# A strip of the last store in three transfers, three quarters of it on eight engines

## Chip, core and metric

One NeuronCore of a Trainium2 chip (trn2). The metric is the device time of one execution in microseconds (us). The profile's span is some 1.8 us shorter than that time. All executions compared below are fast ones, at a granted clock of 1.0; the one exception is named where it comes.

## The reference

```python
x = np.random.randn(32, 3, 256, 256).astype(np.float32)
np.rot90(x, k=2, axes=(-2, -1))       # every 256 x 256 image turned by 180 degrees
```

Turning an image by 180 degrees is the same as reversing its 65,536 values. Input and output have 25.17 MB each. There is no arithmetic: the kernel moves bytes and reverses them.

## The kernel before

The 96 images are cut into three tiles A, Bt and Ct of 32 images (8 MB). An image lies on four partitions, a quarter (E = 16,384 values, 64 KB) on each. The copies reverse every row inside its partition. The store writes the four quarters of an image in turned order. All transfers are issued by SyncE.

```python
    G = 32                      # images in a tile
    E = L // 4                  # 16384 values, 64 KB: one row of a partition
    J = E // 8                  # 2048, columns of one copy
    N = E // 32
    # x4: g (n s) e  (128 rows of 64 KB);   o4: g n s e  (32 images, 4 quarters)

    def load(t, g, lo=0, hi=E):
        nc.sync.dma_start(out=t[:, lo:hi], in_=x4[g][:, lo:hi])

    def store(t, g):
        nc.sync.dma_start(out=o4[g][:, ::-1, :], in_=t[:, :])

    def inside(t):              # 12 copies on VectorE: reverse each row in place
        ...

    load(A, 0, 0, N)            # 2 KB of each row first
    load(A, 0, N, E)
    load(Bt, 1)
    load(Ct, 2)
    for g, t in enumerate((A, Bt, Ct)):
        inside(t)
        store(t, g)
```

## Time and profile before

| | kernel before |
|---|---|
| time | 122.92 us, median of 3 runs (122.79 to 123.21) |
| span of the profile | 121.1 us |
| DMA engines busy | 97.4% of 16 engines' span |
| VectorE busy | 36% |
| last store: issued, landed | 77.6 us, 120.3 us |

The lines themselves are in the prediction below. The trace keeps a record of every packet (start, duration, bytes), and each transfer ends on each of its engines with a packet of 4 bytes (9 ns), and a count of the transfer's semaphore follows it; I call that packet the *closing*. The kernel before has 112 of them for its seven transfers, 16 each, and 16 counts on the semaphore of its last store. A packet starts 3 to 4 ns before the one ahead of it on the same engine ends, and so an engine's packets can be strung together, although a record does not name its engine. Where two engines coincide to a few ns, they can be mistaken for each other.

### The profile page before, as it was taken

The numbers are of one execution on the slowest core, as the hardware profiler recorded it, in microseconds if no ns is written. First come the engines' busy times: TensorE is split into PE (matmuls) and PEld (weight loads), VectorE is DVE, ScalarE is ACT, GpSimd is POOL, SyncE is SP. The second block draws the span as 40 slices with busy tenths as digits, with TensorE's granted clock in tenths as the row PEclk, the third lists the DMA queues.
The fourth block names the chain that finished last, engine by engine and source line by source line (L and its number), as shares of the span: only waits on it lengthen the run. The fifth ranks groups of instructions, "written<-read, shape, count | busy, mean of one in ns | idle before, by whom it ended". The sixth has DMA issues, their size and how long they took to land.

```text
span 121.1 us, 94 instructions
## 1 busy us (share of the span) xinstructions
DVE 44.2 (36%) x36; POOL 0.2 (0%) x4
## 2 busy tenths in 40 slices
DVE  0000000599994199998039999600000000000000
POOL 0000000000000000000000000000000000000000
DMA  9977987897799879978989977997799779977980
GB/s 359 399 336 336 650 356 336 346 693 346 346 411 628 346 346 476 563 346 346 346 346 476 563 346 346 563 476 346 346 584 455 346 346 606 433 346 346 671 368 0
DMA packets 1008, 50.33 MB, mean 416 GB/s; under 512 B 112, under 2 KB 112, under 8 KB 240
## 3 DMA queue, kind: packets, MB, share of 16 engines
q1 hardware_dynamic: 1008, 50.33, 97.4%
HBM read 25.17 MB, written 25.17 MB: 416 GB/s over the span
## 4 chain that ended last, share of the span: by engine, by line
DMA 33%; DVE 25%; another core or an unknown queue 4%; issue 1%; SPq 1%; DVEq 0%
DMA Bt<-in_x_dram 33%; DVE T L53 8%; DVE Ct L53 8%; DVE Bt L53 8%; SPq L56 1%; DVEq L53 0%
## 5 line engine op out<-in xcount | busy, mean ns | idle before, releaser
L53 DVE COPY T<-A 128x2048 f32<-128x2048 f32 x4 | 4.9, 1227 | 22.7 <-DMA A<-in_x_dram 22.6
L53 DVE COPY T<-Ct 128x2048 f32<-128x2048 f32 x4 | 4.9, 1227 | 5.4 <-DMA Ct<-in_x_dram 5.3
L53 DVE COPY T<-Bt 128x2048 f32<-128x2048 f32 x4 | 4.9, 1227 | 4.4 <-DMA Bt<-in_x_dram 4.3
L53 DVE COPY Bt<-T 128x2048 f32<-128x2048 f32 x4 | 4.9, 1227 | 0.1
L53 DVE COPY A<-T 128x2048 f32<-128x2048 f32 x4 | 4.9, 1227 | 0.1
L53 DVE COPY Ct<-Ct 128x2048 f32<-128x2048 f32 x4 | 4.9, 1227 | 0.1
L53 DVE COPY Bt<-Bt 128x2048 f32<-128x2048 f32 x4 | 4.9, 1227 | 0.1
L53 DVE COPY A<-A 128x2048 f32<-128x2048 f32 x4 | 4.9, 1227 | 0.1
L53 DVE COPY Ct<-T 128x2048 f32<-128x2048 f32 x4 | 4.9, 1227 | 0.1
L89 POOL MEMSET const-bfloat16-1.0<- 128x1 bf16 x1 | 0.1, 101 | 0.0
L89 POOL MEMSET const-uint8-127<- 128x1 uint8 x1 | 0.1, 101 | 0.0
L89 POOL MEMSET const-float32-0.0<- 128x1 f32 x1 | 0.1, 98 | 0.2 <-issue 0.2
L89 POOL MEMSET const-float32-1.0<- 128x1 f32 x1 | 0.1, 98 | 0.0
## 6 DMA issues: line engine op xcount, KB each, us to landing
A<-in_x_dram SPq DMA_DIRECT2D x1, 7936.0 KB, 21.4
A<-in_x_dram SPq DMA_DIRECT2D x1, 256.0 KB, 2.8
Bt<-in_x_dram SPq DMA_DIRECT2D x1, 40.3
Ct<-in_x_dram SPq DMA_DIRECT2D x1, 60.3
out_dram<-A SPq DMA_DIRECT2D x1, 43.9
out_dram<-Bt SPq DMA_DIRECT2D x1, 43.8
out_dram<-Ct SPq DMA_DIRECT2D x1, 42.7
```

The source lines that it names most:

```text
L53: tc.keep_in_program_order(nc.vector.tensor_copy(out=dst, in_=src))
L56: nc.sync.dma_start(out=t[:, lo:hi], in_=x4[g][:, lo:hi])
L89: nc = _bacc.Bacc("TRN2", target_bir_lowering=False, num_devices=1)
```

## The change

The intent, as the diff shows it: take 1 KB off the end of each of the 128 rows of the last store, and send these pieces in three transfers that don't use the engines evenly. 64 rows go in 16 groups, twice 32 rows in 8 groups. Eight engines carry 4 + 4 + 4 of the 1 KB pieces and the other eight carry 4. If the first eight end the last store early, this levels them.

```diff
+    M = E // 64                     # 256 values, 1 KB
...
-    def store(t, g):
-        nc.sync.dma_start(out=o4[g][:, ::-1, :], in_=t[:, :])
+    def store(t, g, lo=0, hi=E, i=0, j=G):
+        nc.sync.dma_start(out=o4[g][i:j, ::-1, lo:hi], in_=t[4 * i:4 * j, lo:hi])
...
-    for g, t in enumerate((A, Bt, Ct)):
-        inside(t)
-        store(t, g)
+    inside(A)
+    store(A, 0)
+    inside(Bt)
+    store(Bt, 1)
+    inside(Ct)
+    store(Ct, 2, 0, E - M)
+    store(Ct, 2, E - M, E, 0, 16)
+    store(Ct, 2, E - M, E, 16, 24)
+    store(Ct, 2, E - M, E, 24, 32)
```

## The prediction

> **What bounds the kernel now.** I read four views, in this order: the page's busy shares with its DMA part, the DMA issues, the waits of SyncE's queue, and the stretches of time at the very end.
>
> ```profile
> DVE 44.2 (36%) x36; POOL 0.2 (0%) x4
> ...
> DMA packets 1008, 50.33 MB, mean 416 GB/s; under 512 B 112, under 2 KB 112, under 8 KB 240
> ...
> q1 hardware_dynamic: 1008, 50.33, 97.4%
> ```
>
> VectorE works a third of the span. The 16 DMA engines work 97.4% of it, all from one queue. Every byte has to go in once and out once (25.17 MB each way), so this is a copy at the pace of the DMA engines, and the chain of waits on the page (which names the load of Bt and the copies) is only one of several paths beside it.
>
> ```profile
> out_dram<-A SPq DMA_DIRECT2D x1, 43.9
> out_dram<-Bt SPq DMA_DIRECT2D x1, 43.8
> out_dram<-Ct SPq DMA_DIRECT2D x1, 42.7
> ```
>
> ```profile
> 77.59 0.54 SPq L59 DMA_DIRECT2D out_dram<-Ct  x1
> ```
>
> The last store is issued at 77.59 us (timeline) and lands 42.7 us later, at 120.3, although its own 8 MB take only 19.3 us: it stands behind the stores of A and Bt in the queue. So whatever SyncE issues shortly after 77.6 is issued some 20 us before an engine could start on it.
>
> ```profile
> SPq L100 <- DMA out_dram<-Bt: 19.3, 1, 19.3
> SPq L100 <- DMA out_dram<-Ct: 19.3, 1, 19.3
> SPq L100 <- DMA out_dram<-A: 3.5, 1, 3.5
> ```
>
> At the end SyncE only waits: 19.3 us for the store of Bt, 19.3 us more for that of Ct. The engines run from one 8 MB transfer into the next without a gap, and the end is set by the slowest of 16 engines.
>
> ```profile
> 119.20:119.40 0.20, 0.00 (x0) 0.00 (x0) 1.00 0.00 0
> 119.40:119.50 0.10, 0.00 (x0) 0.00 (x0) 1.00 0.01 0
> 119.50:119.60 0.10, 0.00 (x0) 0.00 (x0) 1.00 0.02 0
> 119.60:119.70 0.10, 0.00 (x0) 0.00 (x0) 1.00 0.01 0
> 119.70:119.80 0.10, 0.00 (x0) 0.00 (x0) 1.00 0.03 0
> 119.80:119.90 0.10, 0.00 (x0) 0.00 (x0) 1.00 0.02 0
> 119.90:120.00 0.10, 0.00 (x0) 0.00 (x0) 1.00 0.01 0
> 120.00:121.10 1.10, 0.00 (x0) 0.00 (x0) 1.00 0.00 0
> ```
>
> This is the part that the change aims at. The last but one column is the DMA share; this view books a packet at one moment, so what is seen here are only the 4-byte packets with which each engine closes the transfer (9 ns each). They are spread over 119.4 to 120.0. In the packet records of the trace the 16 closings end at 119.44, .51, .55, .61, .62, .66, .75, .75, .75, .76, .78, .83, .85, .86, .88 and 119.98; their mean is 119.73. The semaphore counts the last of them 0.34 us after it (120.32), and the barriers that follow end the span 0.8 us after that. If all 16 ended together the span could shrink by 119.98 - 119.73 = 0.25 us, 0.2% of the time. That is the ceiling of any balancing of this store. The records do not say which engine a packet ran on, so which engines are the late ones can't be read.
>
> [...] a 64 KB packet takes 2418 ns, 27.1 GB/s, 434 for 16. [...] Here it is 1.0 us from the first issue (0.73) to the first packet (1.75), and 0.34 us from the last packet to the semaphore; between queued transfers neither is seen. [...]
>
> **The change part by part.** *Duration of a packet.* The trace has three sizes in steady flow: 2 KB 84 ns, 62 KB 2342, 64 KB 2418. (2418 - 84) / 62 = 37.65 ns per KB, and 84 - 2 x 37.65 = 8.7 ns fixed; 62 KB gives 2343, as measured. A packet starts some 3 ns before the one ahead of it ends. So I estimate 1 KB at 46 ns, a pitch of 43, and 63 KB at 2380. A closing packet adds some 6 ns.
>
> *Removed.* 1 KB from each of 128 rows, 8 rows per engine: 8 x 37.65 = 0.30 us less on every engine.
>
> *Added.* The strips of 64, 32 and 32 rows: 4 rows on every engine from the first, 4 + 4 more on engines 0 to 7. Engines 0 to 7: 12 x 43 ns + 3 x 6 ns = 0.53 us. Engines 8 to 15: 4 x 43 + 6 = 0.18 us. Net: engines 0 to 7 end 0.23 us later, engines 8 to 15 end 0.12 us earlier; the mean moves by +0.06 us, which is what the cutting costs.
>
> *Moved.* Nothing in the copies or loads. SyncE issues three more transfers, each some 0.4 to 0.54 us (the seven issues now take 0.39 to 0.63), until about 79.4 us: hidden, as shown above. At the end it has three more semaphores to pass; a wait that is already satisfied costs some 0.05 us (from the last landing to the next instruction it is 0.07 now), perhaps one of them after the last landing.
>
> *What lies on the path.* Only the last closing counts, and it depends on where engines 0 to 7 stand in the list above. (a) They are the 8 early ones: their last goes from 119.75 to 119.98, the others' last from 119.98 to 119.86; the change is 0.0. (b) They are mixed: drawing 8 of the 16 at random, the last closing moves by 0.17 us on average. (c) They are the late ones: +0.23. SyncE's issue of a transfer takes 0.39 us and the first packets of the 16 engines start over 0.36 us[...]. But the first reads took from 81 to 620 ns, which shuffles the order. I take (a) 45%, (b) 45%, (c) 10%: 0.45 x 0 + 0.45 x 0.17 + 0.1 x 0.23 = 0.10 us. [...] The end's waits: 0.03. Sum +0.18 us on 122.92: 123.1.
>
> **Rivals.** *The balance works.* Best case: engines 0 to 7 are the early ones by just the right amount, and the last closing falls by perhaps 0.1 us: 122.8. For it: the spread of 0.54 us is there. Against it: half of the 0.35 us shifted between the halves falls on engines that differ among themselves as much as the halves can; in the list the 8 early ones themselves span 0.31 us, so two groups can't level it.
>
> *A new wait.* The strips write between the rows' ends of the range of the main store. If the program takes the two for overlapping, SyncE waits until the main store has landed (120.3) before it issues the strips: 3 issues of 0.45, 1.0 us to the first packet, 0.2 us of data, 0.34 to land: +2.5 to 3 us, 125.7. Against it: the two pieces of A's load, which also interleave column-wise, are issued at 0.73 and 1.18 with no wait between; but there it is the SBUF side that they share, and the DRAM side only as a read. I give it 3%.
>
> *Small writes to HBM are slow.* 1 KB packets may not keep a pitch of 43 ns: the first 2 KB reads took up to 620 ns. Once running, they took 84. If a 1 KB write cost 100 ns, engines 0 to 7 would end 12 x 57 = 0.7 us later still: 123.8.
>
> *The strips go first.* The columns of the strip are final after the second copy on Ct (65 us), so the order on SyncE's queue could be turned round. Each engine would then carry the same packets in another order: no change of the time.
>
> **Range and chances.** Three runs of the kernel before lie within 0.42 us, more than the effect. Below: the good rival and that scatter, 122.6. Above: slow small packets or the wrong half, 123.6. Also, at 58 us all 16 engines once took 3.2 to 3.8 us for a 64 KB packet, 1.1 us lost; the three runs agree so well that I take it to be in all of them. Faster by over 2% means below 120.5: impossible with an unchanged byte count and 0.25 us to win, 0.01. Slower by over 2% is above 125.4: only the new wait does it, 0.03.
>
> **What would show it.** Packets 1008 + 128 + 32 = 1168, 144 of them under 512 B and 272 under 2 KB. Three issues more, done by about 79.5 us. 1 KB packets of about 46 ns. Of the 144, 16 + 8 + 8 close the strips; it would be 160 if all three used 16 engines. The last closing within -0.1 to +0.4 us of 119.98. I am wrong if SyncE issues a strip after 120 us, if 1 KB packets take 100 ns or more, if the strips of 32 rows use other than 8 engines, or if a gap opens between transfers.

Where a recorded text said of the hardware what no trace or run shows, the passage is cut and the cut marked. One cut took a term out of the sum: +0.18 us was 0.10 for the engines, 0.05 for a longer first strip (cut) and 0.03 for the end's waits. Without the cut term it would be +0.13 us, 123.05.

That a strip of 8 groups goes to eight engines was assumed: the trace before has only transfers with 16 closings. The changed kernel's trace shows 8 for each such strip. Which of the 16 engines these are stands in no record: "engines 0 to 7" in the recorded texts is a name for them and not a measured number. Below they are *the eight*, and the rest *the other eight*.

## The result

| | before | after |
|---|---|---|
| median of 4 runs | 122.94 us (122.79 to 123.21) | 122.99 us (122.96 to 123.14) |
| span of the profile | 121.1 us | 121.2 us |
| last closing (packet records) | 119.98 us | 119.99 us |
| last closing counted by its semaphore | 120.31 us | 120.33 us |

The ratio is 1.0004 with a 95% interval of 0.9985 to 1.0023: no difference that could be told. A ratio here and below is the mean time of one kernel's fast runs over that of the other's fast runs of the same rounds, so it isn't quite the ratio of the medians quoted.

The page of the changed kernel, with the packets and the queue:

```profile
DVE 44.2 (36%) x36; POOL 0.2 (0%) x4
...
DMA packets 1169, 50.33 MB, mean 415 GB/s; under 512 B 145, under 2 KB 273, under 8 KB 401
...
q1 hardware_dynamic: 1168, 50.33, 97.4%
q14 instruction: 1, 0.00, 0.0%
```

The kernel's queue has the 1168 packets that were worked out in advance; the 1169th (24 bytes) is in the queue that the page calls "instruction", and it is also the one too many in each of the three counts of small packets. Of the 145, then, 144 are closings: 112 of seven transfers on 16 engines, 16 for the strip of 64 rows and 8 for each strip of 32. The engines' share is what it was.

Its DMA issues (name, issuing queue, count, KB of each, us to landing):

```profile
out_dram<-Ct SPq DMA_DIRECT2D x1, 8064.0 KB, 42.4
...
out_dram<-Ct SPq DMA_DIRECT2D x1, 64.0 KB, 42.0
out_dram<-Ct SPq DMA_DIRECT2D x2, 32.0 KB
```

Its timeline on SyncE (start, duration):

```profile
77.66 2.93 SPq L62 DMA_DIRECT2D out_dram<-Ct  x4
```

All four pieces are issued between 77.66 and 80.59 us, 40 us before they land. In the instruction records the strips take 0.74, 0.79 and 0.71 us to issue against 0.54 us for the main part: longer than I had assumed, and quite hidden.

The waits of SyncE's queue (line, releaser, us in total, times, longest):

```profile
SPq L109 <- DMA out_dram<-Bt: 19.3, 1, 19.3
SPq L109 <- DMA out_dram<-Ct: 19.2, 1, 19.2
...
SPq L109 <- DMA out_dram<-A: 1.2, 1, 1.2
```

Nothing new waits: still 19.3 us and then 19.2 us for transfers that run back to back. The wait for A's store is shorter by 2.3 us (1.2 against 3.5) only because SyncE comes to it later, having issued more.

The end, in stretches of 0.1 us (the last columns are the DMA share and GB/s; a packet is booked whole where it starts):

```profile
119.20:119.30 0.10, 0.00 (x0) 0.00 (x0) 1.00 0.51 164
119.30:119.40 0.10, 0.00 (x0) 0.00 (x0) 1.00 0.61 205
119.40:119.50 0.10, 0.00 (x0) 0.00 (x0) 1.00 0.82 277
119.50:119.60 0.10, 0.00 (x0) 0.00 (x0) 1.00 0.69 226
119.60:119.70 0.10, 0.00 (x0) 0.00 (x0) 1.00 0.31 103
119.70:119.80 0.10, 0.00 (x0) 0.00 (x0) 1.00 0.22 72
119.80:119.90 0.10, 0.00 (x0) 0.00 (x0) 1.00 0.18 62
119.90:120.00 0.10, 0.00 (x0) 0.00 (x0) 1.00 0.04 10
120.00:121.20 1.20, 0.00 (x0) 0.00 (x0) 1.00 0.00 0
```

Where the kernel before showed only its closings, the small packets are now visible. The engines still stop one after another: a staircase that falls from 0.8 at 119.45 to nothing at 120.0, at the same moment as before. The spread has stayed (the last closings of the 16 engines lie within 0.59 us, against 0.54 before), and so has the end.

Who stopped when? Only eight engines have three strips, so a chain of packets with three tells them from the others. In this execution the eight closed the main part at 119.04, .06, .06, .06, .12, .25, .34 and .47 (mean 119.17), the other eight at 119.23, .29, .39, .39, .41, .49, .54 and .74 (mean 119.44). So the eight really were early, by 0.26 us in the mean. But the last of them trailed its own half by 0.3 us. After the strips the last of the eight ends at 119.99, the last of the other eight at 119.92. Without the cut, the latter would have closed at about 119.74 + 0.30 = 120.04 (an estimate from 8 KB at 37.65 ns each). The levelling thus gained about 0.05 us in this execution. Behind it stands an instruction that was not there before: SyncE's wait for the last strip ends with the count at 120.33 (0.34 us after the closing; 0.32 to 0.40 in the ten traces), and it passes one more, satisfied, wait before it goes on to the end of the program: in the instruction records it gets there 0.13 us after the last count, where it took 0.08 before. That is 0.04 us more. None of these small steps is larger than the scatter from one execution to another: the four profiled kernels in which no store is cut (the one before, and `e5_no_copies_b`, `e6_two_turns` and `e8_swap` below) have their last closing at 119.98, 120.05, 119.89 and 120.09 us.

### The profile page after: what moved, and what is told of

Read it like the earlier page. It is cut to its first block, busy times and chain, and to the rows that moved or that the text cites. A ratio compares the mean times of both kernels' runs of the same rounds, so it can differ in the third digit from the quotient of the medians.

```text
span 121.2 us, 97 instructions
## 1 busy us (share of the span) xinstructions
DVE 44.2 (36%) x36; POOL 0.2 (0%) x4
## 3 DMA queue, kind: packets, MB, share of 16 engines
q1 hardware_dynamic: 1168, 50.33, 97.4%
## 4 chain that ended last, share of the span: by engine, by line
DMA 33%; DVE 24%; another core or an unknown queue 4%; issue 1%; SPq 1%; DVEq 0%
DMA Bt<-in_x_dram 33%; DVE T L56 8%; DVE Bt L56 8%; DVE Ct L56 8%; SPq L59 1%; DVEq L56 0%
```

## The experiments

The theory: 16 engines, none of which pauses between two transfers (99.0% busy from 3 to 119 us in the kernel before), each with a list of packets; the end comes when the slowest list is done. The change shifts 0.35 us from one half to the other, while each half is itself spread by some tenths of a us. The rivals are in the expectations. "Before" in the first four had a median of 122.89 us (122.78 to 123.86, 11 runs in those rounds).

### Cutting without shifting

```diff
     store(Ct, 2, 0, E - M)
-    store(Ct, 2, E - M, E, 0, 16)
-    store(Ct, 2, E - M, E, 16, 24)
-    store(Ct, 2, E - M, E, 24, 32)
+    store(Ct, 2, E - M, E)
```

> The strip as one transfer of 128 rows on all 16 engines: the cutting without the shift. Theory (the slowest engine's packets set the end): each engine gains 8 x (43 - 37.65) + 6 = 0.05 us of packet work, and SyncE perhaps one more wait of 0.06 us at the end: 122.94 + 0.05 to 0.11 = 123.0 to 123.05 us; 8 packets of 1 KB of 46 ns on every engine; the spread of the 16 closings stays some 0.5 to 0.7 us, as without a cut. Rival (the shift to engines 0 to 7 bought something that the cutting took back): this kernel is slower than the changed one by 0.1 to 0.25 us, 123.1 to 123.25. [...]

122.96 us (6 runs, 122.83 to 123.21), ratio 0.9997 (0.9973 to 1.0021). All 128 packets of 1 KB took 46 ns. The last closing was at 120.07 us; the 16 of them spread over 0.55 us. What the further transfer cost is too small for these times to tell. There is no sign that the shift buys 0.1 to 0.25 us over this kernel: the changed one is no faster (122.99, in other rounds). But the interval of this ratio is about 0.3 us wide to either side, so a gain of that size is not excluded by the time alone.

### The shift eight times larger

```diff
-    M = E // 64
+    M = E // 8        # strips of 8 KB
```

> The same three strips, 8 KB wide in place of 1 KB: the shift made 8 times larger. Theory: engines 0 to 7 lose 8 x 8 x 37.65 = 2.41 us and get 12 x (8 x 37.65 + 5) + 0.02 = 3.69, +1.28 us; engines 8 to 15 lose 2.41 and get 4 x 306 + 6 = 1.23, -1.18 us. The latest of engines 0 to 7 stood some 0.28 us ahead of the last of all in the trace of the changed kernel, so the end moves by +1.0 us: 124.0 us (124.3 if they hold the last place). Rival (the queue evens out, the numbers of engines don't matter): 123.0. [...]

124.19 us (4 runs, 123.83 to 124.21), ratio 1.0088 (1.0058 to 1.0119), so +1.1 us by the means and +1.3 by the medians: the theory's 124.0 to 124.3, not 123.0. The profiled execution was the fastest of the four (123.83). The stretches of its end:

```profile
117.50:118.00 0.50, 0.00 (x0) 0.00 (x0) 1.00 1.04 442
118.00:118.50 0.50, 0.00 (x0) 0.00 (x0) 1.00 0.87 361
118.50:119.00 0.50, 0.00 (x0) 0.00 (x0) 1.00 0.50 213
119.00:119.50 0.50, 0.00 (x0) 0.00 (x0) 1.00 0.55 229
119.50:120.00 0.50, 0.00 (x0) 0.00 (x0) 1.00 0.47 197
120.00:120.50 0.50, 0.00 (x0) 0.00 (x0) 1.00 0.54 229
120.50:121.00 0.50, 0.00 (x0) 0.00 (x0) 1.00 0.05 16
```

From about 118.5 us the share is one half: eight engines work and eight have ended. In the records the other eight close between 118.37 and 118.71, the eight between 120.60 and 120.86. This shows directly that the transfers of 8 groups ran on eight engines alone, and that their lists set the end. The latest of the eight closed its main part at 117.17; uncut that would be 117.17 + 8 x 8 x 0.03765 = 119.58, and it ends at 120.86, later by 1.28, exactly the amount worked out.

The first row shows the first strip alone. In 117.5 to 118.0 all data packets that start are those of the first strip, which reads partitions 0 to 63 only, and the engines move 442 GB/s from there (packets are booked whole where they start; 8 KB in each 306 ns on 16 engines come to 428). Every one of the 128 packets of 8 KB took 309 ns, against 8.7 + 8 x 37.65 = 310 worked out from transfers on all 128 partitions. So 16 engines that read half of the partitions were as fast here as on all of them.

### The strips ahead of the main part

```diff
-    store(Ct, 2, 0, E - M)
     store(Ct, 2, E - M, E, 0, 16)
     store(Ct, 2, E - M, E, 16, 24)
     store(Ct, 2, E - M, E, 24, 32)
+    store(Ct, 2, 0, E - M)
```

> The three strips ahead of the main part of Ct's store: the same packets on the same engines, in another order. Theory: no change against the changed kernel, 122.9 to 123.05 us, the closings of the last transfer spread over the same 0.3 to 0.6 us. Rival (what matters is that small packets stand at the very end, with their writes confirmed sooner or later than those of 63 KB): a difference of more than 0.15 us, and another delay than 0.34 us from the last closing to its count.

123.00 us (6 runs, 122.82 to 123.39), ratio 1.0005 (0.9976 to 1.0033). SyncE issued the strips at 65.0 us, as soon as the columns were final, and they were written around 100.7 us, between two large transfers, again 46 ns each. The last closing was at 119.97, and its count 0.33 us later. Neither the order of the packets nor small packets at the very end made a difference that these runs could tell (the interval is about 0.3 us to either side).

### The same cut on the first store

```diff
     inside(A)
-    store(A, 0)
+    store(A, 0, 0, E - M)
+    store(A, 0, E - M, E, 0, 16)
+    store(A, 0, E - M, E, 16, 24)
+    store(A, 0, E - M, E, 24, 32)
     ...
     inside(Ct)
-    store(Ct, 2, 0, E - M)
-    store(Ct, 2, E - M, E, 0, 16)
-    store(Ct, 2, E - M, E, 16, 24)
-    store(Ct, 2, E - M, E, 24, 32)
+    store(Ct, 2)
```

> The same cut on A's store, the first of the three; Ct's goes in one piece. Theory: an engine never waits between transfers, so what it is given early it still lags at the end: the last closing as in the changed kernel within 0.2 us, without the wait behind the last landing (0.06 us): 122.9 to 123.0 us. Rival (the shift only counts in the last transfer): the closings of Ct's store stand as in the kernel before, apart by the 0.05 us of cutting. The landings of the two 8-engine strips also tell which of the engines are early: if 0 to 7 always, the author's premise holds; if they are mixed, it depends on the execution.

122.95 us (6 runs, 122.82 to 123.28), ratio 0.9998 (0.9974 to 1.0023). The 16 closings at the end of A's strips, from 80.89 to 81.33 us, come again at the end of Bt's store 19.3 us later and at the end of Ct's 38.64 us later, with the same gaps to within some ns (81.326 becomes 119.964, 81.312 becomes 119.949). So what an engine is given early it still lags at the end, 39 us later. The last closing was at 119.97 us. I had expected the extra wait at the end to be gone; it was not (SyncE goes on 0.13 us after the last count, as in the changed kernel), since the strips' semaphores are still waited for at the end, one of them after that of Ct's store. No gain in time could be seen.

This execution also bears on the premise: the eight closed the cut store of A at 80.50 to 80.80 (mean 80.68), the other eight at 80.72 to 81.07 (mean 80.94). With 0.26 us here, 0.26 in the changed kernel and 0.24 with strips of 8 KB (means 117.03 and 117.27), the eight were early in each. The trace with the strips first, read in the same way at the end of Bt's store, gives less: 0.19 us (means 100.25 and 100.44). Why they lead was not tested.

### A smaller shift, on the first store

```diff
-    M = E // 64
+    M = 192           # 768 B, on A's store as in the one above
```

> The cut on A's store, with strips of 768 B. In three traces engines 0 to 7 closed the cut store 0.24 to 0.27 us ahead of 8 to 15 in the mean, and the strip of 1 KB shifts 0.35; this one shifts less: engines 0 to 7 8 x -28.2 + 12 x 33 + 18 = +0.19, engines 8 to 15 -226 + 4 x 33 + 6 = -0.09, together 0.28 us. Theory: both halves end level in the mean, but their own spread of 0.4 to 0.6 us stays, so the last closing gains at most 0.1 us: 122.8 to 122.95, not to be told from the kernel before. Rival (a level pair of halves is worth the whole 0.25 us): 122.65 or less.

122.96 us (6 runs, 122.73 to 123.53) against 122.99 for the kernel before in those rounds; ratio 0.9999 (0.9975 to 1.0023). Packets of 768 B took 36 ns. In the profiled execution the eight were ahead by only 0.15 us (means 80.76 and 80.91), so even this shift of 0.28 us was too large for it. The last closing at 119.90 us was the earliest of the kernels with these strips, within the 0.1 us expected; but a kernel without strips reached 119.89 (`e6_two_turns`), and nothing can be told in the time. No version beats the kernel before.

### The delay at 58 us: three more kernels

The prediction counted on a loss of 1.1 us per engine at 58 us as present in every run. It is larger than all that the change moves, so I tried to move it. In the kernel before, in stretches of 2 us:

```profile
55.00:57.00 2.00, 1.97 (x2) 0.00 (x0) 1.00 1.21 524
57.00:59.00 2.00, 0.15 (x1) 0.00 (x0) 1.00 1.78 524
59.00:61.00 2.00, 0.00 (x0) 0.00 (x0) 1.00 0.00 0
```

Each of the first two rows has 16 packets of 64 KB starting in it (524 GB/s), booked as 1.21 and 1.78: 2.42 us each, then 3.56 us each. The kernel after has the same delay at the same time (16 packets of 3.20 to 3.79 us, started at 58.00 to 58.58).

First, Bt's store earlier (the kernel before without the copies on Bt, all stores in one piece):

```diff
-    inside(Bt)
     store(Bt, 1)
```

> No copies on Bt (a wrong result on purpose), so its store is issued at about 42.1 us in place of 57.2. This is about the 1.1 us that every engine loses at 58.0 to 58.5 us, before and after. If it is tied to the arrival of Bt's store in the queue (issued at 57.2, some 1.0 us ahead), it moves to about 43 us, and the total stays at 122.9. If it is tied to the time or to the rows of Ct that are being read then, it stays at 58.0. If it needs the copies that run beside it, it is gone and the total is 121.8.

Bt's store was issued at 41.9 us; the delay stayed at 57.96 to 58.51 us; 123.03 us (4 runs), ratio 1.0009 (0.9985 to 1.0032). It has to do neither with that issue nor with the copies beside it.

Second, against the kernel before, a store between two halves of the last load:

```diff
-    load(Ct, 2)
-    for g, t in enumerate((A, Bt, Ct)):
-        inside(t)
-        store(t, g)
+    load(Ct, 2, 0, E // 2)
+    inside(A)
+    store(A, 0)
+    load(Ct, 2, E // 2, E)
+    inside(Bt)
+    store(Bt, 1)
+    inside(Ct)
+    store(Ct, 2)
```

> The second half of Ct's columns is loaded behind A's store, so the queue runs loads, store, load, stores: two passages from loading to storing in place of one. In all six traces so far the packets that take 1.1 us too long at 58 us are the last one of each engine in the load of Ct, just ahead of the first store's packets, and they stay there when Bt's store is issued 15 us earlier. Theory: passing from loads to stores costs each engine 1.1 us; here it comes at about 51 and again at about 81 us, and the time is 122.9 + 1.1 = 124.0 us. Rival (the time since the start, or the rows read then): one such delay, near 58 us or not at all, and the time stays at 122.9 or falls to 121.8.

122.92 us (4 runs, 122.89 to 123.14), ratio 0.9993 (0.9972 to 1.0014). Its stretches:

```profile
47.00:49.00 2.00, 1.93 (x3) 0.00 (x0) 1.00 1.27 524
49.00:51.00 2.00, 1.93 (x3) 0.00 (x0) 1.00 1.02 262
51.00:53.00 2.00, 1.97 (x2) 0.00 (x0) 1.00 1.21 524
...
79.00:81.00 2.00, 0.00 (x0) 0.00 (x0) 1.00 1.44 623
```

The delay has moved: in 49 to 51 us 16 packets of 32 KB (262 GB/s) are booked as 1.02, 2.04 us each in place of the median of 1.21. The packets just ahead of these are late too, by 0.12 us on average, so that an engine loses 0.96 us here in all. At the second passage from load to store, at 81 us, it does not return (1.44 for 623 GB/s is the normal rate, as 1.21 is for 524). My theory of a cost at each passage is wrong; that of a fixed time is wrong too.

Third, loads and stores of Bt and Ct in turned order:

```diff
-    load(Bt, 1)
     load(Ct, 2)
-    for g, t in enumerate((A, Bt, Ct)):
+    load(Bt, 1)
+    for g, t in ((0, A), (2, Ct), (1, Bt)):
```

> Loads and stores of Bt and Ct in turned order (A, Ct, Bt). The delay of 1.1 us per engine moved to 49.7 to 50.1 us when a store was put in there, and did not come a second time at 80 us, so it is neither a matter of the time nor of each passage. Left are the first passage from loads to stores, and the last rows of Ct as such (in all runs so far the delayed packets read these). First passage: the delay stays at 58 us, now in the load of Bt. Rows of Ct: it moves to about 38.6 us, into the load of Ct. The time stays at 122.9 either way.

One run (state unknown), 123.01 us, with 123.13 for the kernel before beside it.

```profile
37.00:39.00 2.00, 0.71 (x1) 0.00 (x0) 1.00 1.06 459
...
57.00:59.00 2.00, 0.13 (x1) 0.00 (x0) 1.00 1.79 524
```

The delay stays at 58 us, in the load of Bt now, and the rows of Ct are read at the normal rate (1.06 for 459). So it goes with the first passage from loads to stores: the last packet of each engine ahead of the first store (with packets of 32 KB, mostly the last). In every trace but that of `e6_two_turns` these packets took 3.2 to 3.9 us in place of 2.42. Why it happens there and only once stays open.

## Why the prediction was right, point by point

- **The engines bound the kernel and stay the bound.** Right: 97.4% before and after, 412 to 416 GB/s over the span in the profiled kernels, no gap between transfers, 123.1 us predicted and 122.99 measured.
- **The durations.** Right: 46 ns for 1 KB and 2380 ns for 63 KB, both measured as estimated. The shift of 1.28 us in the large version came out to the hundredth.
- **Where the eight stand.** I gave 45% to "the early ones", 45% to "mixed". Four traces with the 1 KB or 8 KB strips show them early by 0.19 to 0.26 us in the mean (0.15 with those of 768 B), but with their slowest members within the others' range: nearer to the first case. It fits that the measured step is smaller than my +0.18 us: +0.02 us on the last count between the two profiled executions, where the sum had 0.10 for the engines, and 0.04 us of waiting behind it. But executions of kernels without strips scatter by 0.2 us in their last closing, so this is not shown.
- **The cut term.** I allowed 0.05 us for a longer first strip; nothing measured stood behind it. It fell away: 442 GB/s from partitions 0 to 63 in `e2_wide8k`, where the strips are 8 KB wide.
- **Issue.** I put the last issue's end at 79.4 us; it was 80.6. The three strips take 0.71 to 0.79 us each to issue, not 0.4 to 0.54. In five traces the ten transfers of 8 groups took 0.69 to 0.79 us to issue, the stores on 16 engines 0.54 to 0.74; that the number of engines alone makes the difference is not shown. It is hidden either way.
- **The end's wait.** I put 0.03 us in the sum; it came and cost 0.04 us.
- **A new wait between strips and main part.** It did not come: all were issued by 80.6 us.
- **Where the hoped-for gain went.** The ceiling was 0.25 us (the closings listed average 119.724, not 119.73; the difference stands), and 8 engines can't be levelled with 8 others by one shift while each half is itself spread over 0.2 to 0.5 us. The shift of 0.35 us also overshoots a lead of 0.26 us. What the levelling gained (an estimated 0.05 us in one execution) the extra wait took back. Each of these sizes is read from single profiled executions; in the times none of them is resolved.
- **What the right time is worth.** Little. Every term of the +0.18 us is smaller than the interval of the result, and a forecast of no change at all would have fitted as well. What was tested is the mechanism behind the sum, and only where it was made large: the shift of 8 KB.

## What to carry to other kernels

When every engine of a transfer queue is busy from start to end, first compute how far the last closing stands behind the mean of all closings: no rebalancing can win more than that, and here it was 0.25 of 123 us. Extra transfers that are issued well ahead of their turn cost nothing here that could be told beyond their packets (46 ns for 1 KB); with three of them one more wait came at the end (0.04 us), with one of them none. A shift between engines kept until the end of the kernel here (39 us later, `e4_cut_a`), so it could stand in an early store as well as in the last.
